# Sliding-window attention units on TensorE: scores ahead of the transposes, one fixed order, steps queued in order

## The chip, the core and the metric

One core of a Trainium2 chip runs one program: TensorE (PE) multiplies, VectorE (DVE) and ScalarE (ACT) do the element-wise work, GpSimd (POOL) small helpers, SyncE (SP) issues the DMAs. The program holds a list of instructions for each engine, with waits on semaphores for what other engines must have finished. The metric is device microseconds of one execution, the median of the runs. The kernel before the change takes 1589.18 us (median of 3 runs, 1588.21 to 1589.36).

## The reference

A decoder block on 1024 tokens of width 1024, in float32:

```python
h = rms_norm(x, ln1_g)
rq, rk, rv, rg, aq, ak, av, gate_a, gate_b = jnp.split(h @ w_in + b_in, SPLIT_IDX, axis=-1)
ry = head_group_norm(retention_chunkwise(rotary(rq), rotary(rk), rv), ret_norm_g)
branch_a = (silu(rg) * ry) @ w_ret_out
ay = sliding_window_sink_attention(rotary(aq), rotary(ak), av, attn_sinks)   # 16 q heads, 2 kv heads of 64
branch_b = ay @ w_attn_out
x = x + (sigmoid(gate_a) * branch_a + sigmoid(gate_b) * branch_b) @ w_out
h2 = rms_norm(x, ln2_g)
x = x + (silu(h2 @ w_ffn_gate) * (h2 @ w_ffn_up)) @ w_ffn_down
return rms_norm(x, lnf_g)
```

The attention works on blocks of 128 queries. A block sees its own 128 keys and the 128 before them (block 0 its own alone), masked to a window of 128, and each head has a learned sink that takes part in the softmax:

```python
m = jnp.maximum(jnp.max(scores, axis=-1, keepdims=True), sink)
e = jnp.exp(scores - m)
probs = e / (jnp.sum(e, axis=-1, keepdims=True) + jnp.exp(sink - m))
out = jnp.einsum('bnhgqk,bnkhd->bnqhgd', probs, vb)
```

## The kernel before, in words

Every float32 operand of a large product is split into a rounded high part and a rest (`split`, `halves`), and a product is three matmuls: high by high, high by low, low by high. The kernel is a row of stages on TensorE: the first norm with k and v, the attention with q's projection and the gates, the retention's v, the retention, the output products, the FFN. The change is in the attention stage alone (L355 to L525, in the trace from about 45 to 357 us).

**The fill.** `quad_q(g)` (L355) projects the queries of four heads (quad g, 0 to 3): 4 products of 24 matmuls of 512 columns, in steps of 3 matmuls (`mm_g`, L148). After each it evicts the bank with an ACT operation (L382); after the third and the fourth it rotates one half of the tokens: six DVE operations, two ACT casts and two DVE rests into the staging tile `stg` (L392 to L401), which goes out to DRAM and comes back in the layout that the scores need, one write (`q_d`, L403) and four reads (L405). `gate(n)` (L482) is a dense product of 48 matmuls, with an ACT tanh (L486) after each half. Weights come by DMA and are split by ACT and DVE (L374, L375 for q; L128, L131 for gates). `Fill` hands these products out a step at a time.

**The units.** There are 32 units (`geo`, L409): unit u is quad u // 8 on block u % 8. A unit has these steps:

- `u_scores` (L417): 8 matmuls of 256 columns, for each of four heads the high and the low part of k against q, into two PSUM tiles "s" (two buffers); by head a DVE operation that adds the mask and takes the row's extreme (L436), and an ACT exponential that sums its row (L439). Then the reciprocal of the sums on DVE (L442), and the scaling of the four heads, two on ACT (L445) and two on DVE (L447).
- `u_transpose` (L451): 8 transposes into two PSUM tiles "t" (two buffers); of each an ACT cast `ph` (L460) and a DVE rest `pl` (L461).
- `u_values` (L464): 4 matmuls of v against `ph` and `pl` into the PSUM tile "pv", which has one buffer. Then two ACT copies (L474, L475) and two DVE additions (L476, L477) out of that bank into `tm`, and an ACT cast and a DVE rest into q's tile (L479, L480).

For block 0 of a quad the scores have 128 columns and there is one transposed tile. The loop (L500) has 33 iterations. Iteration i does `u_transpose(i - 1)`, `u_scores(i)` with all its DVE and ACT work, six or seven steps of fill, and `u_values(i - 1)`. After the loop 120 matmuls of gates remain (`fl.rest()`).

**What sets the order.** The program is traced in that order, and a scheduler then orders each engine's instructions by priority, under their dependencies. `in_order(engines)` (L102) is a context that ties each instruction of an engine to the one traced before it, so that the scheduler can't move them against each other. Before, the attention stage is outside any such context.

Of the kernel before, what the change touches and what calls it, by code (L numbers as in the profile page):

```python
# [2 lines left out]

# [11 lines left out]
ALU = mybir.AluOpType  # L15
# [8 lines left out]
AHEAD = 100  # L24
WARM1 = 30
# [7 lines left out]
def f32(t):  # L33
    return t.bitcast(F32)
# [3 lines left out]
def hybrid_block(ctx: ExitStack, tc: tile.TileContext, x, ln1_g, w_in, b_in, ret_norm_g, w_ret_out,  # L38
# [139 lines left out]

    class Fill:
# [104 lines left out]
    with tc.tile_pool(name="gt", bufs=1, side="right") as gt, tc.tile_pool(name="w1", bufs=1) as w1:  # L284
# [73 lines left out]
        def quad_q(g):  # L358
# [19 lines left out]
            for z, half in ((0, 0), (0, 1), (1, 0), (1, 1)):  # L378
                pt = acc(f"aq{g}{z}{half}")
                yield from mm_g(pt, w[z], H, half * 512)  # L380
                t = r512("ra" if z == 0 else "rb", 2 - z, f"q{g}{z}{half}")
                nc.scalar.activation(t, pt, AF.Identity, bias=bcol[:, QB + 4 * z + g:QB + 4 * z + g + 1], scale=1.0)  # L382
                ab[z, half] = t
                if z == 0:
                    yield
                    continue
                c = slice(half * 512, half * 512 + 512)
                a, b = ab[0, half], t
                stg = w1.tile([P, 4, 512], F32, tag="stg", bufs=1, name=f"stg{g}{half}")
                s0, s1, s2, s3 = (stg[:, i, :] for i in range(4))  # L390
                cos, sin = atab[:, 0, c], atab[:, 1, c]
                nc.vector.tensor_tensor(out=s2, in0=a, in1=cos, op=ALU.mult)  # L392
                nc.vector.tensor_tensor(out=s1, in0=b, in1=sin, op=ALU.mult)
                nc.vector.tensor_tensor(out=s2, in0=s2, in1=s1, op=ALU.subtract)
                nc.vector.tensor_tensor(out=s0, in0=a, in1=sin, op=ALU.mult)
                nc.vector.tensor_tensor(out=s3, in0=b, in1=cos, op=ALU.mult)
                nc.vector.tensor_tensor(out=s3, in0=s3, in1=s0, op=ALU.add)
                nc.scalar.activation(s0.bitcast(F32R), s2, AF.Copy)
                nc.vector.tensor_tensor(out=s2.bitcast(F32R), in0=s2, in1=s0, op=ALU.subtract)
                nc.scalar.activation(s1.bitcast(F32R), s3, AF.Copy)  # L400
                nc.vector.tensor_tensor(out=s3.bitcast(F32R), in0=s3, in1=s1, op=ALU.subtract)  # L401
                qd = q_d[2 * g + half]
                nc.sync.dma_start(qd, stg)  # L403
                for r in range(4):
                    nc.sync.dma_start(f32(Bt[r * 32:r * 32 + 32, jb:jb + 4, c]),  # L405
                                      qd[:, r, :].rearrange("(j e) c -> e j c", e=32))
# [7 lines left out]
        scs = {}  # L414
        phs = {}

        def u_scores(u):  # L417
# [5 lines left out]
            scs[u] = sc  # L423
            nc.gpsimd.tensor_copy(sc[:, :, nk:nk + 1], nsink[:, 4 * g:4 * g + 4].rearrange("p (j o) -> p j o", o=1))  # L424
            nm = tiny.tile([P, 4], F32, tag="nm", name=f"nm{g}{b}")
            den = tiny.tile([P, 4], F32, tag="den", name=f"den{g}{b}")
            for jp in range(2):
# [6 lines left out]
                for jj in range(2):  # L434
                    j = 2 * jp + jj
                    nc.vector.tensor_tensor_reduce(out=sc[:, j, 0:nk], in0=pt[:, jj * 256:jj * 256 + nk], in1=mk,  # L436
                                                   scale=1.0, scalar=nsink[:, 4 * g + j:4 * g + j + 1],
                                                   op0=ALU.add, op1=ALU.min, accum_out=nm[:, j:j + 1])
                    nc.scalar.activation(sc[:, j, 0:nk + 1], sc[:, j, 0:nk + 1], AF.Exp, scale=-1.0,  # L439
                                         bias=nm[:, j:j + 1], accum_out=den[:, j:j + 1])  # L440
            rd = tiny.tile([P, 4], F32, tag="rd", name=f"rd{g}{b}")
            nc.vector.reciprocal(rd, den)  # L442
            for j in range(4):
                if j % 2:
                    nc.scalar.activation(sc[:, j, 0:nk], sc[:, j, 0:nk], AF.Copy, scale=rd[:, j:j + 1])  # L445
                else:
                    nc.vector.tensor_scalar(out=sc[:, j, 0:nk], in0=sc[:, j, 0:nk], scalar1=rd[:, j:j + 1],  # L447
                                            scalar2=None, op0=ALU.mult)

        def u_transpose(u):  # L450
            g, b, nk, Bt, jb, qc = geo(u)  # L451
            sc = scs.pop(u)
            phs[u] = []
            for kb in range(nk // P):
# [5 lines left out]
                nc.scalar.copy(ph, pt)  # L460
                nc.vector.tensor_tensor(out=pl, in0=pt, in1=f32(ph), op=ALU.subtract)  # L461
                phs[u].append((ph, pl))

        def u_values(u):  # L464
# [7 lines left out]
            pvv = pv.rearrange("p (i z q) -> p i z q", i=2, z=2)  # L472
            tm = w1.tile([P, 2, P], F32, tag="tm", bufs=1, name=f"tm{g}{b}")
            nc.scalar.copy(tm[0:64], pvv[64:128, :, 0, :])  # L474
            nc.scalar.copy(tm[64:128], pvv[0:64, :, 1, :])  # L475
            nc.vector.tensor_tensor(out=tm[0:64], in0=pvv[0:64, :, 0, :], in1=tm[0:64], op=ALU.add)  # L476
            nc.vector.tensor_tensor(out=tm[64:128], in0=pvv[64:128, :, 1, :], in1=tm[64:128], op=ALU.add)  # L477
            v = Bt[:, jb:jb + 4, qc].rearrange("p (i z) q -> p i z q", z=2)
            nc.scalar.copy(v[:, :, 0, :], tm)  # L479
            nc.vector.tensor_tensor(out=v[:, :, 1, :], in0=tm, in1=f32(v[:, :, 0, :]), op=ALU.subtract)  # L480
# [19 lines left out]
        for i in range(NU + 1):  # L500
            if i % NB == 0 and 0 < i < NU:
                fl.until(3 * (i // NB - 1) + 1)
            if i > 0:
                u_transpose(i - 1)
            if i < NU:
                u_scores(i)
            fl.step((i + 1) * left // (NU + 1) - i * left // (NU + 1))
            if i > 0:
                u_values(i - 1)
                if i % 4 == 0:  # L510
                    g, b, _, Bt, jb, _ = geo(i - 1)
                    c = slice((b // 4) * 512, (b // 4) * 512 + 512)
                    nc.sync.dma_start(ay_d[g, :, :, c], f32(Bt[:, jb:jb + 4, c]))
            if i == 2 * NB + 4:
                wv = act.tile([P, 16, 512], F32, tag="B", name="wv")
                for q in range(4):
                    nc.sync.dma_start(wv[:, 4 * q:4 * q + 4, :],
                                      w_in[(q // 2) * 512:(q // 2) * 512 + 512, C_RV + (q % 2) * 512:
                                           C_RV + (q % 2) * 512 + 512].rearrange("(k p) n -> p k n", p=P))
            if i > 3 * NB and i % 2:  # L520

                k = (i - 3 * NB) // 2
                nc.vector.tensor_tensor(out=wv[:, 4 + k, :], in0=wv[:, 12 + k, :], in1=wv[:, 4 + k, :],
                                        op=ALU.subtract)
        fl.rest()  # L525
# [1121 lines left out]
```

## Time and profile before

| | |
|---|---|
| median of 3 runs | 1589.18 us |
| the profiled execution | 1587.27 us |
| its span, first to last instruction | 1585.5 us |
| TensorE busy | 1569.7 us |
| VectorE busy | 995.4 us |
| ScalarE busy | 720.2 us |
| mean granted TensorE clock | 0.998 |

The trace covers the profiled execution's span; the 1.8 us beside it lie outside. TensorE's rows need care: a matmul of 512 columns is drawn 0.39 us long, while the next one starts 0.23 us after it, so that a busy TensorE may still be waiting. Start times are exact; ends are modelled.

### The profile page before, as it was taken

What the parts mean: (1) busy time and instruction counts of PE and PEld (TensorE: products, weight loads), DVE (VectorE), ACT (ScalarE), POOL (GpSimd) and SP (SyncE); (2) the same over time, 40 slices, a digit from 0 to 9 for tenths busy, and PEclk for the clock granted to TensorE, in tenths of its full rate; (3) what the DMA queues carried; (4) which work ended last, traced back from release to release, by engine and by line L of the source; (5) the groups of instructions that cost most, each with busy time, mean ns of one, the idle gap of its engine ahead of it and who ended that gap; (6) DMA issues with size and microseconds to landing.
All of it is one profiled execution on the core that took longest, in us unless ns stands there. A gap on an engine that the chain in (4) does not pass through costs nothing.

```text
span 1585.5 us, 20874 instructions
## 1 busy us (share of the span) xinstructions
PE 1569.7 (99%) x7483; PEld 1306.8 (82%) x7483; DVE 995.4 (63%) x1773; ACT 720.2 (45%) x1446; POOL 362.3 (23%) x308
## 2 busy tenths in 40 slices
PE   9999999999999999999999999999999999999998
PEld 8887888888888888888888888888888888788886
DVE  6459978787657663878544368444444444778656
ACT  5258877844233333544221256333333333344445
POOL 2000000000045441000000013555555555200001
PEclk9999999999999999999999999999999999999999
DMA  6564654440364455654545102333333333862333
GB/s 203 161 170 124 206 190 151 145 140 34 126 226 148 134 166 186 231 184 160 176 150 194 54 0 79 101 108 111 108 100 104 107 109 100 306 226 86 99 104 123
DMA packets 148886, 223.13 MB, mean 141 GB/s; under 512 B 9195, under 2 KB 81709, under 8 KB 147246
## 3 DMA queue, kind: packets, MB, share of 16 engines
q1 hardware_dynamic: 148782, 221.80, 43.1%
q8 instruction: 59, 0.97, 0.2%
q14 instruction: 45, 0.37, 0.1%
HBM read 149.67 MB, written 67.37 MB: 137 GB/s over the span
## 4 chain that ended last, share of the span: by engine, by line
PE 88%; ACT 5%; DVE 5%; issue 1%; DMA 0%; POOL 0%; POOLq 0%; SPq 0%; DVEq 0%; ACTq 0%
PE fA L1310 15%; PE fB L1310 8%; PE dA L1571 7%; PE wA L814 7%; PE dxP L1571 6%; PE fC L1310 4%; PE wB L814 3%; PE va L659 3%; PE vP L659 2%; ACT sc L439 2%; PE acc_g L155 2%; PE acc_g L156 2%; PE wo L1248 2%; PE wo L1249 2%; PE acc_ba L156 2%; PE acc_ba L157 2%
## 5 line engine op out<-in xcount | busy, mean ns | idle before, releaser
L1571 PE MATMUL dA<-dwP,daP 128*128 128x512 f32 x528 | 121.4, 390 | 0.8 <-DVE xf L1347 0.8
L1571 PEld LDWEIGHTS dA<-dwP,daP 128*128 128x128 f32 x528 | 98.8, 188 | 22.7 <-DVE xf L1347 1.2
L1571 PE MATMUL dxP<-dwP,daP 128*128 128x512 f32 x396 | 90.2, 389 | 0.0
L1571 PEld LDWEIGHTS dxP<-dwP,daP 128*128 128x128 f32 x396 | 74.3, 188 | 15.4
L424 POOL COPY sc<-nsink 128x4 f32<-128x4 f32 x32 | 12.7, 399 | 275.2 <-PE pT L457 147.4
L1368 POOL TENSOR_TENSOR xf<-xf 128x512 f32<-128x512 f32 x44 | 67.9, 1543 | 33.0 <-issue 30.1
L156 PE MATMUL acc_g<-h,wh_g 128*128 128x512 f32 x192 | 75.4, 393 | 0.0
L155 PE MATMUL acc_g<-h,wh_g 128*128 128x512 f32 x192 | 75.3, 392 | 0.0
L157 PE MATMUL acc_g<-h,wl_g 128*128 128x512 f32 x192 | 75.2, 392 | 0.0
L439 ACT ACTIVATE sc<-sc,nm 128x257 f32<-128x257 f32 (+1 forms) x128 | 62.5, 492 | 26.0 <-DVE nm L436 25.6
L1321 POOL TENSOR_TENSOR xf<-xf 128x512 f32<-128x512 f32 x33 | 49.3, 1493 | 54.5 <-ACT t_1P L128 22.4
L436 DVE CUSTOM_DVE_ANT_0 sc<-s,amask,nsink 128x256 f32<-128x256 f32 (+1 forms) x128 | 54.1, 461 | 9.5 <-PE s L433 9.2
L1331 ACT COPY xf<-fA 128x512 f32<-128x512 f32 x44 | 25.7, 586 | 74.3 <-PE fA L1310 74.3
L131 DVE TENSOR_TENSOR dwP<-wd,dwP 128x512 fp32r<-128x512 f32 x77 | 56.0, 728 | 4.6 <-ACT dwP L128 4.6
L128 ACT CAST dwP<-wd 128x512 fp32r<-128x512 f32 x77 | 47.4, 615 | 12.4 <-PE dA L1571 9.9
L155 PE MATMUL acc_bb<-ay,wh_bb 128*128 128x512 f32 x128 | 50.9, 399 | 0.0
L156 PE MATMUL acc_bb<-ay,wh_bb 128*128 128x512 f32 x128 | 50.3, 393 | 0.0
L156 PE MATMUL aq<-h,wh_aq 128*128 128x512 f32 x128 | 50.2, 392 | 0.0
L155 PE MATMUL aq<-h,wh_aq 128*128 128x512 f32 x128 | 50.1, 391 | 0.0
L1489 POOL TENSOR_TENSOR rs_f<-tot,mhalf 128x1 f32<-128x1 f32 x8 | 4.8, 605 | 198.0 <-DVE tot L1486 198.0
L157 PE MATMUL acc_bb<-ay,wl_bb 128*128 128x512 f32 x128 | 50.0, 391 | 0.0
L157 PE MATMUL aq<-h,wl_aq 128*128 128x512 f32 x128 | 50.0, 392 | 0.0
(799 smaller groups left out, 4395.5 us busy)
## 6 DMA issues: line engine op xcount, KB each, us to landing
act_d<-xf SPq DMA_DIRECT2D x77, 256.0 KB, 2.1
daP<-act_d SPq DMA_DIRECT2D x21, 512.0 KB
q_d<-stg SPq DMA_DIRECT2D x8, 1024.0 KB
q<-q_d SPq DMA_DIRECT2D x32, 256.0 KB, 6.2
ay_d<-q SPq DMA_DIRECT2D x8, 1024.0 KB
ay<-ay_d SPq DMA_DIRECT2D x4, 2048.0 KB, 13.9
wr_daP<-act_d SPq DMA_DIRECT2D x14, 512.0 KB, 3.9
wr_g<-in_w_in SPq DMA_DIRECT2D x12, 512.0 KB, 5.9
```

Of the source, the lines that this page charges most:

```text
L131: nc.vector.tensor_tensor(out=lo, in0=raw, in1=f32(hi), op=ALU.subtract)
L155: nc.tensor.matmul(pt, hi[:, k, :], xh, start=(k == 0), stop=False)
L156: nc.tensor.matmul(pt, hi[:, k, :], xl, start=False, stop=False)
L157: nc.tensor.matmul(pt, lo[:, k, :], xh, start=False, stop=(k == 7))
L436: nc.vector.tensor_tensor_reduce(out=sc[:, j, 0:nk], in0=pt[:, jj * 256:jj * 256 + nk], in1=mk, scale=1.0, scalar=nsink[:, 4 * g + j:4 * g ...
L439: nc.scalar.activation(sc[:, j, 0:nk + 1], sc[:, j, 0:nk + 1], AF.Exp, scale=-1.0, bias=nm[:, j:j + 1], accum_out=den[:, j:j + 1])
L659: nc.tensor.matmul(vbanks[pr][tt], x_[:, c], w[:, u, :], start=(fresh and k + z == 0), stop=(k == 3 and z == 2), skip_group_check=not fresh)
L814: nc.tensor.matmul(pt, o[:, w, k, :], v, start=(first and k + z == 0), stop=(k == 3 and z == 2), skip_group_check=not first)
L1310: nc.tensor.matmul(pt, o[:, w, k, :], v, start=(first and k + z == 0), stop=(k == 3 and z == 2), skip_group_check=not first)
L1321: nc.gpsimd.tensor_tensor(out=dst[q], in0=dst[q], in1=sg[q], op=ALU.mult)
L1368: nc.gpsimd.tensor_tensor(out=o, in0=a, in1=b, op=op)
L1571: nc.tensor.matmul(banks[tt], a[:, u, c], w[:, v, :], start=(fresh and f + z == 0), stop=(f == NP - 1 and z == 2), skip_group_check=not fresh)
```

## The change

Six edits, all in the attention stage.

1. The loop runs in `in_order(nc.tensor.engine)`: TensorE keeps the traced order.
2. Iteration i now traces `u_scores(i)`, one step of fill (`FIRST`), `u_transpose(i - 1)`, `u_scale(i)`, `u_out(i - 2)`, the other steps of fill, and `u_values(i - 1)`.
3. `u_scale` is the second half of the old `u_scores` (reciprocal and scaling); `u_out` is the second half of the old `u_values` (all that reads the bank "pv"). It is traced an iteration later than before, behind the scaling of the unit two further on.
4. Each DVE and ACT operation of a unit goes through `queued`, which ties it to the engine's queued operation before it. Evictions, splits and the rotation are not tied.
5. The rotation of quads 1 to 3 is put in a list, `beside`, and one entry is issued after each step of fill; the write and reads through DRAM come with the last entry. Quad 0 is rotated at once, as before.
6. The write of four finished blocks (`ay_d`) is issued from `u_out`.

```diff
+        def queued(x):
+
+            i = x.ins
+            if i.engine in queues:
+                tc.add_manual_dep(i, queues[i.engine],
+                                  mybir.DependencyInfo(mybir.DependencyClass.NoSync, mybir.DependencyReason.DATA),
+                                  reason="queued")
+            queues[i.engine] = i.name
...
                 try:
                     next(self.gens[0])
                     n -= 1
+                    if beside:
+                        beside.pop(0)()
...
+                todo = [partial(mix, s2, a, cos, ALU.mult), partial(mix, s1, b, sin, ALU.mult),
+                        partial(mix, s2, s2, s1, ALU.subtract), partial(mix, s0, a, sin, ALU.mult),
+                        partial(mix, s3, b, cos, ALU.mult), partial(mix, s3, s3, s0, ALU.add),
+                        partial(hl, s2, s0), partial(hl, s3, s1), ship]
+                if g == 0:
+                    for f in todo:
+                        f()
+                else:
+                    beside.extend(todo[:-2] + [lambda x=todo[-2], y=todo[-1]: (x(), y())])
...
+        def u_out(u):
+            g, b, nk, Bt, jb, qc = geo(u)
+            pvv = pvs.pop(u).rearrange("p (i z q) -> p i z q", i=2, z=2)
             tm = w1.tile([P, 2, P], F32, tag="tm", bufs=1, name=f"tm{g}{b}")
...
+            queued(nc.scalar.copy(tm[0:64], pvv[64:128, :, 0, :]))
+            queued(nc.scalar.copy(tm[64:128], pvv[0:64, :, 1, :]))
+            queued(nc.vector.tensor_tensor(out=tm[0:64], in0=pvv[0:64, :, 0, :], in1=tm[0:64], op=ALU.add))
+            queued(nc.vector.tensor_tensor(out=tm[64:128], in0=pvv[64:128, :, 1, :], in1=tm[64:128], op=ALU.add))
...
+        with in_order(nc.tensor.engine):
+            for i in range(NU + 1):
+                n = (i + 1) * left // (NU + 1) - i * left // (NU + 1)
+                if i % NB == 0 and 0 < i < NU:
+                    fl.until(3 * (i // NB - 1) + 1)
+                if i < NU:
+                    u_scores(i)
+                if i > 0:
+                    fl.step(FIRST)
+                    u_transpose(i - 1)
+                if i < NU:
+                    u_scale(i)
+                if i > 1:
+                    u_out(i - 2)
+                fl.step(n - FIRST if i > 0 else n)
+                if i > 0:
+                    u_values(i - 1)
...
+            u_out(NU - 1)
+            fl.rest()
```

In the rows of the program below a name carries the quad and the block: `sc34` is the score tile of quad 3, block 4 (unit 28), `pv33` the value bank of the unit before it. Rows of the changed program have its own line numbers.

TensorE before, from the values of unit 26 to the fill after the scores of unit 28: `pv` are values, `pT` transposes, `s340` and `s341` the two score tiles, `acc_g13` the fill.

```order
L470 MATMUL pv32_3259<-ph321_3196,vst_169 128x512
L471 MATMUL pv32_3259<-pl321_3197,vst_169 128x512
L457 MATMUL pT330_3272<-ident_81,sc33_3200 128x128 x4
L457 MATMUL pT331_3281<-ident_81,sc33_3200 128x128 x4
L432 MATMUL s340_3294<-kst_168,q2_1418 128x256
L433 MATMUL s340_3294<-kst_168,q2_1418 128x256
```

TensorE in the changed program at the same place:

```order
L499 MATMUL pv32_3259<-ph321_3214,vst_169 128x512
L500 MATMUL pv32_3259<-pl321_3215,vst_169 128x512
L457 MATMUL s340_3269<-kst_168,q2_1418 128x256
L458 MATMUL s340_3269<-kst_168,q2_1418 128x256
...
L160 MATMUL acc_g13_0_3243<-h1_112,wl_g13_3240 128x512
L486 MATMUL pT330_3290<-ident_81,sc33_3175 128x128 x4
L486 MATMUL pT331_3299<-ident_81,sc33_3175 128x128 x4
```

The scores of unit 28 now stand directly behind the values of unit 26, and one step of fill is between them and the transposes of unit 27; 18 matmuls of fill and the values of unit 27 follow.

ScalarE before, in the iterations of unit 27 and 28: exponentials and scaling (`sc`), copies out of the value bank (`tm`), casts of the transposed tiles (`ph`), the last cast (`q2`), a gate's tanh (`tb`).

```order
L445 ACTIVATE sc33_3200<-sc33_3200,rd33_3222 128x256 x2
L474 COPY tm32_3264<-pv32_3259 64x256
L475 COPY tm32_3264<-pv32_3259 64x256
L460 CAST ph330_3277<-pT330_3272 128x512
L460 CAST ph331_3286<-pT331_3281 128x512
L479 CAST q2_1418<-tm32_3264 128x2x128
L439 ACTIVATE sc34_3290,den34_3293<-sc34_3290,nm34_3292 128x257 x4
L486 ACTIVATE tb130_3327<-acc_g13_0_3243,bhalf_87 128x512
L445 ACTIVATE sc34_3290<-sc34_3290,rd34_3312 128x256 x2
```

ScalarE in the changed program, the iteration of unit 28:

```order
L464 ACTIVATE sc34_3265,den34_3268<-sc34_3265,nm34_3267 128x257 x4
L489 CAST ph330_3295<-pT330_3290 128x512
L489 CAST ph331_3304<-pT331_3299 128x512
L522 ACTIVATE tb130_3327<-acc_g13_0_3243,bhalf_87 128x512
L474 ACTIVATE sc34_3265<-sc34_3265,rd34_3308 128x256 x2
L507 COPY tm32_3314<-pv32_3259 64x256
L508 COPY tm32_3314<-pv32_3259 64x256
L512 CAST q2_1418<-tm32_3314 128x2x128
```

The copies of unit 26's values (`tm32`) stood ahead of the exponentials of unit 28; they now stand behind them, behind the casts of unit 27 and behind unit 28's scaling. VectorE has the same order: its additions of `tm32` (L509, L510) follow unit 28's four reductions (L461), unit 27's two rests (L490), unit 28's reciprocal (L471) and its scaling (L476).

VectorE in the changed program where a rotation meets the units, between the end of iteration 2 and the third reduction of iteration 3 (`stg11` is the rotation of quad 1's second half, `tm00` the end of unit 0, `sc03` and `nm03` unit 3's reductions):

```order
L510 TENSOR_TENSOR tm00_1055<-pv00_1002,tm00_1055 64x256
L402 TENSOR_TENSOR stg11_989<-q101_852,atab_164 128x512
L402 TENSOR_TENSOR stg11_989<-q111_987,atab_164 128x512
L513 TENSOR_TENSOR q0_627<-tm00_1055,q0_627 128x2x128
L402 TENSOR_TENSOR stg11_989<-stg11_989 128x512
L402 TENSOR_TENSOR stg11_989<-q101_852,atab_164 128x512
L402 TENSOR_TENSOR stg11_989<-q111_987,atab_164 128x512
L461 ISA sc03_1100,nm03_1102<-s030_1104,amask_166,nsink_85 128x256
L461 ISA nm03_1102 128x1
L402 TENSOR_TENSOR stg11_989<-stg11_989 128x512
L461 ISA sc03_1100,nm03_1102<-s030_1104,amask_166,nsink_85 128x256
```

Five rotation operations stand between unit 0's last use of the value bank and unit 3's first reduction, a sixth behind that. Two rests of the rotation (L406) follow ahead of unit 3's fourth reduction.

Unit 0's scores stand, in the changed program, behind 156 matmuls of q's projection; before they stood behind all 192 of quads 0 and 1 and 41 matmuls of a gate.

More of the change, by code (lines that the diff above doesn't have):

```diff
@@ L2 @@
 from contextlib import ExitStack, contextmanager
+from functools import partial
 import numpy as np
@@ L24 @@
 AHEAD = 100
+FIRST = 1
 WARM1 = 30
@@ L177, in dense @@
         run(dense_g(src, col, X, evac, name))
+    beside = []
     class Fill:
@@ L391, in quad_q @@
                 cos, sin = atab[:, 0, c], atab[:, 1, c]
[L392 to L406, printed above, removed]
+                def mix(o, p, q, op):
+                    nc.vector.tensor_tensor(out=o, in0=p, in1=q, op=op)
@@ new lines, in hl, with ship @@
+                def hl(v, hi):
+                    nc.scalar.activation(hi.bitcast(F32R), v, AF.Copy)
+                    nc.vector.tensor_tensor(out=v.bitcast(F32R), in0=v, in1=hi, op=ALU.subtract)
+                def ship(qd=q_d[2 * g + half], stg=stg, Bt=Bt, jb=jb, c=c):
+                    nc.sync.dma_start(qd, stg)
+                    for r in range(4):
+                        nc.sync.dma_start(f32(Bt[r * 32:r * 32 + 32, jb:jb + 4, c]),
+                                          qd[:, r, :].rearrange("(j e) c -> e j c", e=32))
@@ L426, in u_scores @@
             den = tiny.tile([P, 4], F32, tag="den", name=f"den{g}{b}")
+            scs[u] = sc, den
             for jp in range(2):
@@ L499, in hybrid_block @@
         left = 32 * 8 - 8 - 20
[L500 to L524, printed above, removed]
```

56 lines of the change are left out of this document (33 added, 23 removed).

## Prediction

> **What bounds the kernel now.** I read the page first, then the chain of waits, TensorE's waits in the attention stage, that stage's windows, and the timeline of one regular stretch.
>
> ```profile
> span 1585.5 us, 20874 instructions
> PE 1569.7 (99%) x7483; PEld 1306.8 (82%) x7483; DVE 995.4 (63%) x1773; ACT 720.2 (45%) x1446; POOL 362.3 (23%) x308
> ```
>
> TensorE is the bound, and the change takes no matmul away. All it can win is time in which TensorE waits. The windows, with the attention stage as 100 to 330 us (columns: busy time of PE, PEld, DVE, ACT, POOL, then the granted clock):
>
> ```profile
> 0.00:40.00 40.00, 36.42 (x267) 32.99 (x268) 26.44 (x46) 23.24 (x41) 11.72 (x25) 0.96 0.61 205
> 100.00:330.00 230.00, 226.62 (x1208) 187.58 (x1208) 194.01 (x574) 189.72 (x528) 12.39 (x30) 1.00 0.52 161
> ```
>
> TensorE shows 3.4 us idle in the stage, with 84% of VectorE and 82% of ScalarE used. The modelled ends hide more: a 512-column row is drawn 0.39 us and the next starts 0.23 us on, so each wait may hide 0.16 us; with two waits a unit at most, 64 x 0.16 = 10.2 us, which makes 3.4 to 13.6 us. I take 8 us as what the old order loses, the middle.
>
> The late part of the stage is regular. TensorE's rows there, unit 27's values to unit 28's:
>
> ```profile
> 301.27 0.40 PE L470 MATMUL pv<-ph,vst 128*128 128x512 f32 x1
> ...
> 303.20 0.28 PE L433 MATMUL s<-kst,q 128*128 128x256 f32 x1
> ...
> 303.91 0.28 PE L433 MATMUL s<-kst,q 128*128 128x256 f32 x1
> ...
> 308.81 0.40 PE L470 MATMUL pv<-ph,vst 128*128 128x512 f32 x1
> ...
> 309.74 1.03 PE L457 MATMUL pT<-ident,sc 128*128 128x128 f32 x8
> ```
>
> An iteration takes 308.81 - 301.27 = 7.54 us, and 0.93 of it (308.81 to 309.74) are the four value matmuls. TensorE does not wait there. So in the new order, with the same work, TensorE would come to the values 7.54 - 0.93 = 6.61 us after the first score matmul.
>
> **The change part by part.** *The order and the moved output step (edits 1 to 4).* The values of unit i-1 write the one bank "pv". In iteration i the old contents, unit i-2's, are read by two ACT copies and two DVE additions, and the rows of the order put these behind unit i's exponentials and scaling. Unit i's exponentials need unit i's scores, and TensorE's next scores now come behind these values. That closes a ring: scores of i, softmax of i, output of i-2, values of i-1, scores of i+1. If it is longer than 7.54 us, it sets the pace, and with TensorE's order fixed no fill can slip in. I add it up from the start of the scores, taking starts of rows that follow each other.
>
> ```profile
> 100.94 0.28 PE L433 MATMUL s<-kst,q 128*128 128x256 f32 x1
> ...
> 101.26 0.48 DVE L436 CUSTOM_DVE_ANT_0 sc<-s,amask,nsink 128x256 f32<-128x256 f32 x1 [0.30 <-PE s L433]
> ...
> 102.27 0.17 DVE L442 RECIPROCAL rd<-den 128x4 f32<-128x4 f32 x1
> ...
> 102.47 0.70 ACT L445 ACTIVATE sc<-sc,rd 128x128 f32<-128x128 f32 x2
> ```
>
> ```profile
> 302.78 0.36 ACT L475 COPY tm<-pv 64x256 f32<-64x256 f32 x1
> 303.17 1.07 ACT L460 CAST ph<-pT 128x512 fp32r<-128x512 f32 x2
> 303.18 0.42 DVE L476 TENSOR_TENSOR tm<-pv,tm 64x256 f32<-64x256 f32 x1 [1.55 <-ACT tm L475]
> 303.61 0.43 DVE L477 TENSOR_TENSOR tm<-pv,tm 64x256 f32<-64x256 f32 x1
> 304.07 0.69 DVE L461 TENSOR_TENSOR pl<-pT,ph 128x512 fp32r<-128x512 f32 x1
> 304.13 0.42 ACT L479 CAST q<-tm 128x256 fp32r<-128x256 f32 x1
> 304.67 0.42 DVE L480 TENSOR_TENSOR q<-tm,q 128x256 fp32r<-128x256 f32 x1
> 305.61 0.48 DVE L436 CUSTOM_DVE_ANT_0 sc<-s,amask,nsink 128x256 f32<-128x256 f32 x1
> 306.19 0.51 ACT L439 ACTIVATE sc<-sc,nm 128x257 f32<-128x257 f32 x1 [1.64 <-DVE nm L436]
> 308.18 0.67 ACT L486 ACTIVATE tb<-acc_g,bhalf 128x512 f32<-128x512 f32 x1
> 308.75 0.90 ACT L445 ACTIVATE sc<-sc,rd 128x256 f32<-128x256 f32 x2
> 309.55 1.03 ACT L128 CAST wh_g<-wr_g 128x1024 fp32r<-128x1024 f32 x1
> 310.60 0.37 ACT L474 COPY tm<-pv 64x256 f32<-64x256 f32 x1
> 310.98 0.37 ACT L475 COPY tm<-pv 64x256 f32<-64x256 f32 x1
> ```
>
> - Scores run 0.118 us apart (303.20 to 303.91, six steps). The fourth closes the first score tile: 3 x 0.118 + 0.28, and 0.04 to the DVE (101.22 to 101.26). First reduction at 0.67.
> - First exponential 0.58 later (305.61 to 306.19): 1.25. Four take 1.99 of ACT (306.19 to 308.18): 3.24. Unit i-1's transposes are long done.
> - The casts `ph` of unit i-1: ACT is free 0.96 later (303.17 to 304.13), the first is done after 0.59 (1.07 less the 0.48 step). First rest `pl` at 3.24 + 0.59 + 0.04 = 3.87. Two rests of 0.60 (304.07 to 304.67): the reciprocal of unit i starts at 5.07.
> - 0.20 to ACT's scaling (102.27 to 102.47): 5.27. Two scalings 0.80 (308.75 to 309.55): 6.07. Two copies, 0.38 (310.60 to 310.98) and 0.36: 6.81.
> - 0.04 (303.14 to 303.18), two additions of 0.43: 7.71.
>
> From there to TensorE there is one row pair, which ends one of TensorE's own waits:
>
> ```profile
> 145.14 0.44 DVE tm L477
> ...
> 145.71 0.47 PE pv L470
> ```
>
> That is 0.13 us after the addition's end (145.58): the values start at 7.84, where TensorE could at 6.61. The iteration takes 7.84 + 0.93 = 8.77 us in place of 7.54: 1.23 us more. Thirty iterations (2 to 31) have the ring. In six it is lighter (three with 128-column scores, three with one transposed tile); between 0 and 1.23 I take half. 24 x 1.23 + 6 x 0.62 = 33.2 us. Iterations 11 and 22 have six steps of fill, so TensorE arrives 3 x 0.227 = 0.68 us earlier for nothing: 1.4 more, 34.6 us. An error of 0.25 us in the ring is 7 us.
>
> *The rotation (edit 5).* Six halves of eight DVE operations at 0.60 us:
>
> ```profile
> 104.61 0.60 DVE stg L396
> 105.22 0.60 DVE pl L461
> ```
>
> That is 28.8 us of VectorE if all of it lay on the ring, and 0 if all of it fell into VectorE's pauses there. Worked for iteration 2 into 3 by the order's rows: after the second addition (7.71) stand five rotations and unit 0's last rest, 5 x 0.60 + 0.35, so unit 3's first reduction can start at 11.06, where the ring wants it at 8.77 + 0.67 = 9.44: 1.6 us late. Three more stand between its four reductions, 1.8 us. So 3.4 us a quad, 10 us in three; other places fall into the pause ahead of `pl` and cost nothing.
>
> *Other fill on the ring.* Evictions and weight splits aren't tied, but take their place in the lists. A tanh (0.57, 308.18 to 308.75) between the casts and the scaling fits into ACT's pause there (3.24 + 0.96 = 4.20 to 5.27); a pair of weight splits of quads 2 and 3 doesn't always. Four such pairs at up to 1.2 us and some eight evictions at 0.57: 0 to 9.4 us. I take 6.
>
> *Unit 0 earlier.* Its scores now stand 36 matmuls ahead of the end of quad 1's projection.
>
> ```profile
> 77.00 1.77 SPq L405 DMA_DIRECT2D q<-q_d  x4
> ```
>
> ```profile
> 89.67 0.39 PE L157 MATMUL aq<-h,wl_aq 128*128 128x512 f32 x1
> ```
>
> ```profile
> q<-q_d SPq DMA_DIRECT2D x8, 256.0 KB, 6.2
> ```
>
> The row at 89.67 is the last of the 192, so TensorE reaches unit 0 at 89.90 - 36 x 0.227 = 81.7. The four reads of q were issued from 77.0 to 78.8, the last at about 78.3, and land 6.2 us later: 84.5. The DMA queue ahead of them is unchanged. A wait of 2.8 us that was not there (0 to 4). Later quads have whole iterations of cover, and edit 6 has the 120 gate matmuls behind the loop (120 x 0.227 = 27 us).
>
> Sum: 34.6 + 10 + 6 + 2.8 - 8 = +45 us. The profiled execution's 1587.3 becomes 1632; the median lies 1.9 above it, so **1634 us**.
>
> One rule of the Trainium skill speaks of such waits. The rows first: the granted clock is 0.96 in the first 40 us, where TensorE idles 3.6 us, and 1.00 in the stage with its short waits. "TensorE: Matmul & The Clock Gate", section "HAM oscillation", warns of idle gaps over about 3.4 us, after which the clock is halved for a window. By that rule the ring's 1.23 us is harmless, and only iterations like 3 (1.2 + 3.4) would lose half of such a window, a further 1.7 us each, an estimate of 3 to 5 us in all and a time of about 1638; no run shown so far has such a gap, and none of it is in the sum.
>
> **The rivals.**
>
> *A, faster: the ring is shorter than 6.61 us.* Then TensorE never waits for the bank, the 8 us go, unit 0 costs 2.8: 1589.2 - 5.2 = 1584 us. For it: VectorE idles 1.55 us and ScalarE 1.64 us in the regular stretch, so the engines have room. Against: these are pauses in sequence; ACT's own work from the first exponential to the last copy is 1.99 + 0.96 + 0.80 + 0.74 = 4.5 us, and with the 1.25 before and the 1.03 behind it 6.8, without any pause for `pl`. It decides if my sum is 1.23 too long. Chance 0.09.
>
> *B, the ring binds lightly.* At 7.0 in place of 7.84 it costs 30 x 0.4 = 12, with fill in the pauses, unit 0 at 2.8, less 8: +7, about 1596 us. It needs handoffs half as long as the rows show. Chance 0.09, of which half lies within 0.2% of the old time if the old waits were nearer 13.6.
>
> *C, VectorE binds.* With the rotation all on the ring: +19 on the forecast, 1653 us. Chance 0.07.
>
> That the change does not do what it says is excluded by the rows of the order.
>
> **How the numbers follow.** The forecast has 0.75; slower takes in C and half of B: 0.75 + 0.07 + 0.045, rounded 0.87; faster 0.09; same 0.04. (0.2% of this time, 3.2 us, is about what a measurement can tell.) The range: below, 27 (ring 0.25 shorter) + 2 - 13.6 = +15, 1604; above, 42 + 20 + 6 + 2.8 - 3.4 = +67, 1656. It holds the forecast's 0.75 and most of C.
>
> **What would show it.** Right: TensorE's waits led by the first value matmul on the second addition, about 30 times and 1.2 us each; the regular iteration at 8.8 us; ScalarE's copies of unit i-2 behind the scaling of unit i; one wait of unit 0's scores on q's reads near 82 us; the stage some 45 us longer, all after it only shifted. Wrong: iterations of 7.5 us, or waits that sit on the transposes in place of the values, would say that the ring isn't there; long waits on first reductions behind rotations would say that VectorE's load, not the ring, is the price.

## The result and the profile after

The changed kernel takes 1651.57 us (median of 4 runs, 1650.68 to 1651.73), the kernel before 1588.89 us in the same job (4 runs, 1588.21 to 1589.36): a ratio of 1.04, 95% interval 1.0388 to 1.0413. The profiled execution's span is 1649.8 us, 64.3 more than before.

The page, then TensorE's waits (us in all, times, the longest):

```profile
span 1649.8 us, 20928 instructions
PE 1582.7 (96%) x7483; PEld 1316.0 (80%) x7483; DVE 994.2 (60%) x1773; ACT 723.3 (44%) x1446; POOL 358.9 (22%) x308
```

```profile
PE pv L499 <- DVE tm L510: 48.8, 29, 4.4
PE s L457 <- DMA q<-q_d: 3.3, 1, 3.3
```

One wait carries nearly all: the first value matmul on the second addition out of the bank "pv", 29 times. The same stage's windows as before, with the stretch around unit 0 ahead of them (busy time of PE, PEld, DVE, ACT, POOL, then the granted clock):

```profile
80.00:100.00 20.00, 16.72 (x71) 13.78 (x70) 12.54 (x34) 8.56 (x25) 0.19 (x1) 0.83 0.79 210
100.00:330.00 230.00, 191.21 (x967) 156.98 (x966) 155.27 (x443) 148.10 (x403) 6.43 (x24) 0.96 0.42 135
```

VectorE and ScalarE are less used than before (155 and 148 us of 230, against 194 and 190): neither is full, they wait for each other. And the granted clock, 1.00 in this stage before, is 0.96. A regular iteration:

```profile
351.89 0.47 PE L499 MATMUL pv<-ph,vst 128*128 128x512 f32 x1 [1.71 <-DVE tm L510]
...
352.89 0.28 PE L457 MATMUL s<-kst,q 128*128 128x256 f32 x1
...
353.67 0.48 DVE L461 CUSTOM_DVE_ANT_0 sc<-s,amask,nsink 128x256 f32<-128x256 f32 x1 [1.03 <-PE s L458]
...
354.26 0.51 ACT L464 ACTIVATE sc<-sc,nm 128x257 f32<-128x257 f32 x1 [2.08 <-DVE nm L461]
...
356.25 1.05 ACT L489 CAST ph<-pT 128x512 fp32r<-128x512 f32 x2
...
356.85 1.29 DVE L490 TENSOR_TENSOR pl<-pT,ph 128x512 fp32r<-128x512 f32 x2 [1.47 <-ACT ph L489]
...
358.05 0.17 DVE L471 RECIPROCAL rd<-den 128x4 f32<-128x4 f32 x1
...
358.31 0.91 ACT L474 ACTIVATE sc<-sc,rd 128x256 f32<-128x256 f32 x2 [0.43 <-DVE rd L471]
...
359.25 0.37 ACT L507 COPY tm<-pv 64x256 f32<-64x256 f32 x1
...
360.02 0.42 DVE L509 TENSOR_TENSOR tm<-pv,tm 64x256 f32<-64x256 f32 x1 [1.16 <-ACT tm L508]
...
360.45 0.43 DVE L510 TENSOR_TENSOR tm<-pv,tm 64x256 f32<-64x256 f32 x1
...
361.03 0.47 PE L499 MATMUL pv<-ph,vst 128*128 128x512 f32 x1 [1.35 <-DVE tm L510]
```

Read down, this is the ring step by step: each row waits for the one above it or stands behind it in its engine's queue. Once around takes 361.03 - 351.89 = 9.14 us, where an iteration took 7.54 before. There are two kinds of loss in it: the wait itself, and what follows some of the longer waits. TensorE behind the pause that ends at 294.90:

```profile
294.90 0.64 PE L499 MATMUL pv<-ph,vst 128*128 128x512 f32 x1 [3.76 <-DVE tm L510]
295.34 0.63 PE L500 MATMUL pv<-pl,vst 128*128 128x512 f32 x1
295.76 0.63 PE L499 MATMUL pv<-ph,vst 128*128 128x512 f32 x1
...
298.32 0.45 PE L158 MATMUL acc_g<-h,wh_g 128*128 128x512 f32 x1
298.61 0.40 PE L159 MATMUL acc_g<-h,wh_g 128*128 128x512 f32 x1
298.85 0.40 PE L160 MATMUL acc_g<-h,wl_g 128*128 128x512 f32 x1
```

From 294.90 to 298.32 the matmuls run at half rate: the 512-column ones start 0.42 us apart in place of 0.24 behind that.

**Where the time went.** I take every step between starts of TensorE's rows from 60 to 420 us, less its regular length (0.227 us behind 512 columns, 0.118 behind 256, 0.11 behind a transpose). Steps some 0.2 us too long (0.1 for the short ones) that come five or more in a row are "half rate"; the number of such stretches is in brackets. "Ahead of values" is what stands ahead of a unit's first value matmul; waits ahead of its three others are under "all other".

| us | time | ahead of values | unit 0's scores | half rate | all other | sum |
|---|---|---|---|---|---|---|
| before | 1588.9 | 1.4 | 0 | 0 | 9.7 | 11.1 |
| changed | 1651.6 | 53.8 | 3.4 | 11.8 (6) | 4.2 | 73.2 |

The sums differ by 62.1 us, the medians by 62.7, so nearly the whole difference lies in this stage. Of the 64.3 us between the two profiled executions 2.0 lie ahead of it: the first product of q's projection starts at 47.79 us in place of 45.76, and the granted clock over the first 40 us is 0.91 in place of 0.96.

### The profile page after: what moved, and what is told of

It reads as the page before. It is cut to its first block, busy times and chain, and to the rows that moved or that the text cites. A ratio compares the mean times of both kernels' runs of the same rounds, so it can differ in the third digit from the quotient of the medians.

```text
span 1649.8 us, 20928 instructions
## 1 busy us (share of the span) xinstructions
PE 1582.7 (96%) x7483; PEld 1316.0 (80%) x7483; DVE 994.2 (60%) x1773; ACT 723.3 (44%) x1446; POOL 358.9 (22%) x308
## 4 chain that ended last, share of the span: by engine, by line
PE 83%; ACT 6%; DVE 6%; issue 2%; DMA 2%; SPq 0%; POOL 0%; ACTq 0%; POOLq 0%; DVEq 0%
PE fA L1350 14%; PE fB L1350 7%; PE dA L1611 7%; PE wA L854 6%; PE dxP L1611 5%; PE fC L1350 4%; PE wB L854 3%; PE va L699 3%; PE vP L699 2%; PE wo L1290 2%; PE acc_ba L158 2%; PE acc_ba L160 2%; PE wo L1289 2%; PE wo L1288 2%; PE acc_ba L159 2%
## 5 line engine op out<-in xcount | busy, mean ns | idle before, releaser
L464 ACT ACTIVATE sc<-sc,nm 128x257 f32<-128x257 f32 (+1 forms) x128 | 62.1, 487 | 67.3 <-DVE nm L461 67.3
L448 POOL COPY sc<-nsink 128x4 f32<-128x4 f32 x32 | 7.9, 249 | 340.6 <-PE pT L486 160.1
L499 PE MATMUL pv<-ph,vst 128*128 128x512 f32 x60 | 27.0, 450 | 48.9 <-DVE tm L510 48.8
L461 DVE CUSTOM_DVE_ANT_0 sc<-s,amask,nsink 128x256 f32<-128x256 f32 (+1 forms) x128 | 52.8, 464 | 26.5 <-PE s L458 26.2
L490 DVE TENSOR_TENSOR pl<-pT,ph 128x512 fp32r<-128x512 f32 x60 | 38.8, 686 | 39.0 <-ACT ph L489 38.8
L499 PEld LDWEIGHTS pv<-ph,vst 128*128 128x128 f32 x60 | 11.6, 193 | 62.2 <-ACT tm L508 43.1
L158 PE MATMUL aq<-h,wh_aq 128*128 128x512 f32 x128 | 52.6, 411 | 0.0
L159 PE MATMUL aq<-h,wh_aq 128*128 128x512 f32 x128 | 51.3, 401 | 0.0
L158 PE MATMUL acc_bb<-ay,wh_bb 128*128 128x512 f32 x128 | 50.9, 399 | 0.0
```

The source lines that it names most:

```text
L158: nc.tensor.matmul(pt, hi[:, k, :], xh, start=(k == 0), stop=False)
L159: nc.tensor.matmul(pt, hi[:, k, :], xl, start=False, stop=False)
L461: queued(nc.vector.tensor_tensor_reduce(out=sc[:, j, 0:nk], in0=pt[:, jj * 256:jj * 256 + nk], in1=mk, scale=1.0, scalar=nsink[:, 4 * g + ...
L464: queued(nc.scalar.activation(sc[:, j, 0:nk + 1], sc[:, j, 0:nk + 1], AF.Exp, scale=-1.0, bias=nm[:, j:j + 1], accum_out=den[:, j:j + 1]))
```

## The experiments

Twelve runs, in four jobs. The kernel before took 1589.07 us in the first, 1587.8 to 1588.0 in the others. Each edit is against the changed kernel if nothing else is said.

**Two value banks** (`banks`): odd units' values go into a bank of the fill's pool.

```diff
-            pv = ps("pv", 1, f"pv{g}{b}")
+            pv = ps("pv", 1, f"pv{g}{b}") if u % 2 == 0 else acc(f"pv{g}{b}")
```

> The changed kernel with a second value bank: odd units write their values into one of the three banks of the fill's products, so that the values of unit i-1 wait for the output of unit i-3 and no longer for that of unit i-2. TensorE's order is the same word for word. The ring theory (the bank closes a ring through the softmax of the next unit but one): the 48.8 us of waits of the value matmuls on the second addition go, and with them most of the slow-clock matmuls behind the long waits, some 8 us; left are unit 0's wait of 3.3 us and what was lost before. 1651.6 - 49 - 8 gives 1595 us, 1585 to 1605. The rival that VectorE's and ScalarE's load, with the rotation in it, sets the pace whatever bank is free: the waits move to the rests and scalings, and it stays above 1630 us.

Measured: 1617.9 us, ratio 1.0189 (1.0172 to 1.0206), less than the changed kernel by 33.7 us and more than the theory had. TensorE's waits, then the start of one iteration:

```profile
PE pv L499 <- ACT ph L489: 9.1, 9, 1.8
PE pv L500 <- DVE pl L490: 5.4, 20, 0.6
```

```profile
321.11 0.28 PE L457 MATMUL s<-kst,q 128*128 128x256 f32 x1
...
321.29 0.91 ACT L474 ACTIVATE sc<-sc,rd 128x256 f32<-128x256 f32 x2
...
322.23 0.37 ACT L507 COPY tm<-pv 64x256 f32<-64x256 f32 x1
...
323.89 0.41 ACT L512 CAST q<-tm 128x256 fp32r<-128x256 f32 x1 [0.92 <-DVE tm L510]
...
324.33 0.42 DVE L513 TENSOR_TENSOR q<-tm,q 128x256 fp32r<-128x256 f32 x1 [0.47 <-ACT q L512]
...
324.78 0.48 DVE L461 CUSTOM_DVE_ANT_0 sc<-s,amask,nsink 128x256 f32<-128x256 f32 x1
...
329.64 0.28 PE L457 MATMUL s<-kst,q 128*128 128x256 f32 x1
```

The waits on the additions are gone: the bank's ring was real. But an iteration still takes 8.53 us. Scores that begin at 321.11 could be reduced 0.7 us later; the first reduction starts at 324.78. Ahead of it in VectorE's queue stand the additions and the rest of the older unit's output, which wait for ScalarE's copies and cast, and these for the scaling. So a second ring lies under the first and has no bank in it: scaling, copies, additions, cast, rest, next reductions, exponentials, casts, rests, next scaling, handed to and fro between two engines that keep their order.

**The output at once again** (`now`), tied as it is, right behind its own unit's values; and **between scores and transposes** (`early`).

```diff
-                if i > 1:
-                    u_out(i - 2)
...
                     u_values(i - 1)
+                    u_out(i - 1)
```

> The changed kernel with one step put back: each unit's output step is issued behind its values, as in the kernel before, with the one value bank; TensorE's order, the queued steps and the spread rotation stay. The ring theory: the output is then over 1.9 us behind the values and no softmax is in its way; the softmax starts 1.9 us later and the rests end at about 7.2 us after the scores, where the last value matmul needs them at 7.3. So TensorE hardly waits in a plain iteration, but has little slack: 1590 to 1605 us. The rival of the engines' load: still above 1630 us.

```diff
                 if i < NU:
                     u_scores(i)
+                if i > 1:
+                    u_out(i - 2)
                 if i > 0:
                     fl.step(FIRST)
```

> The changed kernel with the output step of unit i-2 put between unit i's exponentials and the casts of unit i-1's transposes; all else as changed. The ring theory: the bank comes free about 5.1 us after the scores in place of 8.0, ahead of the values at 6.6, but the rests of unit i-1 now end at about 7.3, so that the fourth value matmul waits 0.1 to 0.5 us in an iteration: 1595 to 1612 us. The rival of the engines' load: above 1630 us.

Measured: 1623.22 us, 1.0216 (1.0201 to 1.0232), and 1620.78 us (one run). Both miss their range by over 8 us. TensorE's waits in `now`:

```profile
PE pv L499 <- ACT ph L489: 11.0, 11, 2.8
PE pv L500 <- DVE pl L490: 7.2, 24, 1.1
```

At three tied places the output costs 32 to 63 us over before; earlier helps, but where it is tied to stand ahead of the next unit's work, that work waits instead. In `now`, scores that begin at 318.06 meet a VectorE whose queue holds the older unit's additions and its rest, which waits for ScalarE's cast; the first reduction starts at 321.34, directly behind that rest.

**The rotation in one heap** (`rot`): edit 5 undone.

```diff
-                if g == 0:
+                if g >= 0:
```

> The changed kernel with the rotation of all quads issued at once, as in the kernel before (edit 5 undone); the ring stays. The ring theory: the plain iteration stays at 9.1 us and the waits on the second addition stay near 49 us, 5 more or less, since the same 48 operations come in other places: 1640 to 1660 us. The rival that the spread rotation is the price: 1610 to 1630 us.

Measured: 1664.82 us (one run), 13 more than the changed kernel, just above the range. The pauses ahead of the values grow by only 2.8 us in all (56.6 against 53.8), but are less even, up to 5.2 us, and the stretches at half rate go from 6 to 11: 21.0 us in place of 11.8. So 9.2 of the 13 us hang on which pauses are followed by half rate, and in a single execution that is in part chance (see below).

**No ties** (`noq`), and **no ties with two banks** (`banks_noq`).

```diff
-            if i.engine in queues:
+            if False:
```

> The changed kernel without the ties among the units' VectorE and ScalarE operations; TensorE's order and the one bank stay. Theory (two rings: the bank, and under it the tied order of the two queues, in which the casts ph of unit i-1 stand behind all four exponentials of unit i): with the ties gone casts and rests may go ahead of the next unit's exponentials, both rings get shorter, 1595 to 1625 us, and TensorE's waits on VectorE's additions are under half of the 48.8 us. Rival one (the traced order alone sets the queues, the ties add nothing): 1648 to 1655, waits as before. Rival two (without the ties the output of unit i-2 drifts behind evictions and rotation): over 1660.

> Two value banks and no ties; TensorE's order, the later output and the spread rotation stay. Theory (two rings): both are gone, what is left is unit 0's wait on q's reads (3.4 us, some 3 more at a lower clock) and a little more: 1588 to 1602 us, and TensorE's waits for casts and rests (14.5 us with two banks and the ties) are under 6 us. Rival one (with two banks it is the fixed order of TensorE alone that still waits for the transposes' casts, whatever the two queues do): 1613 to 1621, the same as two banks with the ties. Rival two (VectorE's load): the same 1613 to 1621, with waits on VectorE's rests.

Measured: 1599.97 us, 1.0076 (1.006 to 1.0091), and 1588.47 us, 1.0002 (0.9993 to 1.0011). Both lie in the theory's ranges. With two banks TensorE's waits are:

```profile
PE s L457 <- DMA q<-q_d: 3.5, 1, 3.5
PE pv L500 <- DVE pl L490: 2.1, 3, 1.2
```

So fixing TensorE's order with the scores ahead costs nothing on balance here, once the two other queues and the bank let it run.

**The spread rotation alone, in the kernel before** (`before_rot`), and **TensorE's fixed order alone, in the kernel before** (`before_pe`): `with in_order(nc.tensor.engine):` around the old loop.

```diff
+                    if beside:
+                        beside.pop(0)()
...
+                if g == 0:
+                    for f in todo:
+                        f()
+                else:
+                    beside.extend(todo[:-2] + [lambda x=todo[-2], y=todo[-1]: (x(), y())])
```

> The kernel before with the spread rotation alone. If spreading saves here too (undoing it in the changed kernel cost 13 us), by taking the eight VectorE operations out of one heap: 1578 to 1586 us, at most the 8 us that the old order was said to lose. If the 13 us were only the ring's (a heap of rotations delays a ring that already sets the pace) and the old order, in which fill covers them, loses nothing to it: 1587 to 1591. If each entry of the rotation issued between steps of fill is in the units' way: 1592 to 1600.

> The kernel before with one edit alone: TensorE's traced order held (transposes of i-1, scores of i, fill, values of i-1), the output read out of the bank at once. If the queues' order and the bank are the whole price: unit 0's wait on q's reads is all that is left of the change, 3 to 7 us, 1589 to 1597 us. If holding TensorE's order is itself a price, since fill can no longer slip in where a unit's step is late: 1600 to 1625, with waits spread over casts, rests and scaled scores.

Measured: 1586.74 us, 0.9993 (0.9984 to 1.0002), no difference: in the old order it is the same whether the rotation is spread or not, and the 13 us belong to the kernel with the ring; and 1606.18 us, 1.0116 (1.0102 to 1.0131), the second reading. The waits of `before_pe`:

```profile
PE pT L457 <- DVE sc L447: 8.8, 6, 3.8
PE pT L457 <- ACT sc L445: 4.0, 4, 2.9
```

In the old traced order (transposes, then scores) a fixed TensorE waits for the scaled scores, where the free one before took fill. No wait of a transpose on a scaled score is among the changed kernel's: with the scores ahead of the transposes, the scaling is done when TensorE comes to them.

**Only the output untied** (`out_free`), with one bank and with two (`banks_out_free`): of the units' operations the six of `u_out` go without `queued`, all others stay tied.

```diff
-            queued(nc.scalar.copy(tm[0:64], pvv[64:128, :, 0, :]))
+            nc.scalar.copy(tm[0:64], pvv[64:128, :, 0, :])
...
```

> The changed kernel with the six operations of the output (two copies, two additions, cast and rest of q) not tied; reductions, exponentials, casts, rests and scalings stay tied, as do TensorE's order and the one bank. With all ties off the time was 1600.0 us. Theory (the place of the output is the whole price of the ties: tied, its copies stand behind the scaling of the unit two further on, and its last two operations ahead of the next unit's reductions): 1597 to 1607 us. Rival (the ties among reductions, exponentials, casts and scalings cost as well, for a pair of splits or an eviction can no longer be passed): 1615 to 1640, with waits for casts and rests.

> Two value banks and the output's six operations not tied, all else as changed. Two banks with the ties took 1617.9, without any tie 1588.5 us. Theory (the second ring, too, closes through the output: scaling, copies, additions, cast and rest of q, next unit's reductions, each waiting for the other engine): 1587 to 1597 us. Rival (the second ring is the casts of unit i-1 behind the exponentials of unit i, which stay tied): 1608 to 1620, with TensorE's waits on casts and rests at 14 us as with two banks and all ties.

Measured: 1593.33 us, 1.0034 (1.0022 to 1.0047), less than the theory had, and 1593.33 us, 1.0036 (1.0023 to 1.005), in its range. Untying six operations out of twenty-three gives back 58.2 of the 62.7 us, and a second bank adds nothing to it. `out_free`'s waits ahead of the values, beside unit 0's, and one iteration:

```profile
PE pv L499 <- ACT ph L489: 1.9, 2, 1.2
PE pv L499 <- DVE tm L510: 1.8, 2, 1.6
```

```profile
316.06 0.48 DVE L461 CUSTOM_DVE_ANT_0 sc<-s,amask,nsink 128x256 f32<-128x256 f32 x1 [1.05 <-PE s L458]
...
317.69 0.42 DVE L509 TENSOR_TENSOR tm<-pv,tm 64x256 f32<-64x256 f32 x1
...
318.12 0.43 DVE L510 TENSOR_TENSOR tm<-pv,tm 64x256 f32<-64x256 f32 x1
...
321.91 0.40 PE L499 MATMUL pv<-ph,vst 128*128 128x512 f32 x1
...
323.04 0.37 ACT L507 COPY tm<-pv 64x256 f32<-64x256 f32 x1 [0.85 <-PE pv L500]
...
323.62 0.48 DVE L461 CUSTOM_DVE_ANT_0 sc<-s,amask,nsink 128x256 f32<-128x256 f32 x1 [2.17 <-PE s L458]
```

Left free, the scheduler puts the copies ahead of the next exponentials, into ScalarE's pause while TensorE computes the scores (323.04), and the additions behind the four reductions, into VectorE's pause while ScalarE takes the exponentials (317.69). The bank is free at 318.55, 3.4 us before the values at 321.91, and the iteration is 7.56 us again (316.06 to 323.62).

**Unit 0 later** (`banks_noq_late`): 18 matmuls of the fill move ahead of unit 0, on top of `banks_noq`.

```diff
-        fl.step(20)
-        left = 32 * 8 - 8 - 20
+        fl.step(26)
+        left = 32 * 8 - 8 - 26
```

> Two value banks, no ties, and unit 0's scores 18 matmuls (4.1 us) later in the fill; TensorE's order and the spread rotation stay. Without the last edit 1588.5 us, with one wait of 3.6 us for q's reads and some eight matmuls at half rate behind it (2 us). Theory (that wait and the half rate behind it are all that is left of the change's price): the wait is gone, 1581.5 to 1585 us, faster than both kernels. Rival (18 matmuls less of fill for the units make other waits): 1586 to 1591, with new waits before the values or behind the loop.

Measured: 1588.98 us, 1.0006 (0.9997 to 1.0016): the rival was right.

```profile
PE pv L500 <- DVE pl L490: 3.8, 3, 2.8
PE pT L486 <- DVE sc L476: 2.5, 1, 2.5
```

The wait on q's reads is gone, but unit 0's transposes now wait 2.5 us for its scaling, with a few matmuls at half rate behind that (0.43 us apart from 97.30 to 99.01), and one unit's values wait 2.8 for a rest; TensorE's pauses sum to 10.9 us, against 10.4 without this edit and 11.1 before the change. No version here is faster than the kernel before by more than the measurement can tell.

**The output untied and the rotation in one heap** (`out_free_rot`): both edits above.

> The changed kernel with the output's six operations not tied (1593.3 us) and, besides, the rotation issued in one heap again as before. Undoing the spreading alone, with the ties, cost 13 us, and the heap's iterations there had pauses of 3.5 to 5.2 us ahead of the values. Theory (a heap costs only where the ring already sets the pace): 1590 to 1597 us. Rival (eight VectorE operations in one heap delay the fixed order of TensorE whatever the output does): 1602 to 1610, with pauses over 3 us in the three iterations with a heap.

Measured: 1594.58 us, 1.0043 (1.0026 to 1.006), against 1593.33 with the spread rotation. Outside a ring the heap costs next to nothing.

The same account of TensorE's pauses for the runs that decide (of the 21.2 us under "all other" with two banks, 15.1 are ahead of a unit's later value matmuls, where it waits for casts and rests):

| us | time | ahead of values | unit 0's scores | half rate | all other | sum |
|---|---|---|---|---|---|---|
| two banks | 1617.9 | 11.8 | 3.5 | 3.6 (3) | 21.2 | 40.2 |
| no ties | 1600.0 | 10.3 | 3.7 | 7.2 (3) | 1.9 | 23.1 |
| output untied | 1593.3 | 4.3 | 3.5 | 2.9 (2) | 4.9 | 15.6 |
| two banks, no ties | 1588.5 | 0.0 | 3.6 | 1.5 (1) | 5.2 | 10.4 |
| before, fixed TensorE | 1606.2 | 0.0 | 3.6 | 7.1 (4) | 19.7 | 30.3 |
| rotation in one heap | 1664.8 | 56.6 | 3.6 | 21.0 (11) | 5.1 | 86.3 |

## Why the prediction was right, and by how much it missed

The forecast was 1634 us; 1651.6 were measured, 17.6 more. Step by step:

- **The ring: right in place and mechanism, a little short.** 29 waits of the first value matmul on the second addition, the copies behind the scaling of the unit two further on, 9.14 us a plain iteration against 8.77. Measured from the first score matmul (352.89), the first reduction starts at 0.78 (forecast 0.67), the first exponential at 1.37 (1.25), the rests at 3.96 (3.87), the scaling at 5.42 (5.27), the copies at 6.36 (6.07, ScalarE's two scalings with their handoffs take 0.94, not 0.80), the additions at 7.13 (6.85), the values at 8.14 (7.84). The four value matmuls take 1.00, not 0.93.
- **Rotation and other fill: about right together.** Ring, rotation and fill were put at 34.6 + 10 + 6 = 50.6 us; the pauses ahead of the values are 53.8. With the plain ring at 1.5 us of pause (24 x 1.5, six at half, and 1.4 as in the forecast: 41.9) some 12 remain for rotation and fill, forecast 16. That the total comes so near is in part luck: the plain ring was put 7 us too low, and rotation and fill 4 too high. The iteration worked out in the prediction came as told, with rotations (L402) and their rests (L406) ahead of and between the reductions of unit 3:

```profile
112.18 1.28 DVE L402 TENSOR_TENSOR stg<-q,atab 128x512 f32<-128x512 f32 x2
...
113.50 0.48 DVE L461 CUSTOM_DVE_ANT_0 sc<-s,amask,nsink 128x256 f32<-128x256 f32 x1
...
113.91 0.69 DVE L402 TENSOR_TENSOR stg<-stg 128x512 f32<-128x512 f32 x1
...
115.32 1.29 DVE L406 TENSOR_TENSOR stg<-stg 128x512 fp32r<-128x512 f32 x2
...
116.53 0.48 DVE L461 CUSTOM_DVE_ANT_0 sc<-s,amask,nsink 128x256 f32<-128x256 f32 x1
...
122.33 0.77 PE L499 MATMUL pv<-ph,vst 128*128 128x512 f32 x1 [4.41 <-DVE tm L510]
```

  Its pause is 4.6 us, 3.1 over the plain 1.5, where 3.4 was forecast. But the prediction booked this under edit 5, the spreading. The runs correct that: the rotation lies on the ring in either form, spreading it went with 13 us less there (`rot`, one execution, 9.2 of them half rate) and with next to nothing elsewhere (none in `before_rot`, 1.3 us in `out_free_rot`).
- **Unit 0's scores: right.** 3.4 us against 2.8.
- **The old waits: nearly.** Of 8 us that were to go, 5.5 went: the pauses at all other places fell from 9.7 to 4.2 us.
- **The half rate: the term that failed.** It was left out of the sum, with 3 to 5 us beside it; it is 11.8, two thirds of the miss. The rows of the windows are above (0.96 over the stage, 0.83 around unit 0), and six stretches follow the waits that end at 87.25, 122.33, 236.23, 273.09, 294.90 and 332.39. Three of them follow pauses of only 2.1 to 2.4 us, and two of these (236.23 and 332.39) stand in iterations without any rotation. By the Trainium skill ("TensorE: Matmul & The Clock Gate", section "HAM oscillation"), gaps over about 3.4 us bring the half rate. The stretch shown above lasts 3.42 us, as long as the window that page gives (3.4 us), but the threshold does not hold here: 2.1 us was enough at 332.39. Nor does the length alone decide: a pause of 3.0 us in `out_free_rot` (at 257.48) left the next values 0.23 to 0.31 us apart, at full rate. The same page, section "What's actually happening", says that the window runs free of the program. The traces agree: in each run the granted clock changes only on a grid of 3.413 us. In the changed kernel the half rate of this stage begins at 86.82, 120.95, 237.00, 274.55, 295.03 and 332.58, which are 10, 34, 11, 6 and 11 such steps apart, and from run to run the grid lies elsewhere against the program, 0.1 to 2.7 us behind the span's start. What counts is how much pause falls into one window of this grid (in these rows PE's busy time, the second number, is 3.41 us in a window without a pause, and hides some 0.16 us of each pause; the clock stands third from the end):

```profile
329.17:332.58 3.41, 1.50 (x7) 0.97 (x6) 1.87 (x6) 1.95 (x5) 0.00 (x0) 1.00 0.00 0
332.58:335.99 3.41, 3.41 (x13) 3.01 (x13) 2.00 (x8) 1.09 (x5) 0.00 (x0) 0.50 0.50 195
148.26:151.67 3.41, 1.99 (x9) 1.31 (x7) 2.34 (x6) 2.78 (x7) 0.00 (x0) 1.00 0.23 62
151.67:155.08 3.41, 2.29 (x14) 2.09 (x15) 1.76 (x6) 0.50 (x2) 0.00 (x0) 1.00 1.05 328
155.08:158.49 3.41, 3.41 (x21) 2.87 (x20) 1.95 (x9) 3.03 (x10) 0.19 (x1) 1.00 0.00 0
```

  The pause of 2.1 us that ends at 332.39 lies whole in one window, and the next window is at half rate. The pause of 2.7 us that ends at 152.79 is longer, but the grid cuts it at 151.67 into 1.6 and 1.1 us, and no half rate follows; that of 3.0 us in `out_free_rot` is cut into 1.8 and 1.3. In the changed kernel six windows at full rate hold over 2.0 us of pause in all, and half rate follows each of them; no other is followed by it, and the fullest of these holds 1.96 us. In `rot` it is eleven windows, and 1.88 us. So for pauses of 2 to 3 us it is chance whether they cost twice.
- **The rivals.** A and B fell with the ring. C's time (1653) is nearest to the measured one, but not its mechanism: VectorE is busy 155 of 230 us, less than before, and TensorE's waits don't lie on reductions.
- **What the prediction did not see** cost it nothing, but would have misled a repair: it took 7.54 us for what an iteration needs once the bank is free. Under the bank's ring stood the second one of 8.53 us through the same tied output. A second bank alone gives back 33.7 of 62.7 us; untying the output opens both rings. Which of its six ties matters most was not tried: with the output traced early but tied (`now`) copies stand ahead of the next exponentials on ScalarE as in `out_free`, and it still takes 1623 us, which points to the additions ahead of the reductions and to the cast and rest ahead of the next unit's softmax. One iteration of its trace, told above, has just that; how much each tie costs is not shown.

## What to carry to other kernels

When queues are fixed in order, follow one iteration's work from engine to engine until it comes back to where it began: the longest such loop is the pace, however idle every engine is, and opening one loop shows the next. Tie only what has to be tied: a piece of work with slack, such as an output, is worth most when it may fall into whichever pause comes. And a wait of TensorE can cost more than its length, so look at the start distances behind it too.

## What the runs showed of the hardware

Pauses of TensorE of 2.1 to 4.6 us were followed by stretches of 11 to 18 matmuls in the changed kernel at half rate (0.427 us between 512-column matmuls in place of 0.227), about 2 us lost each time: 6 of them in the changed kernel and 11 in `rot`, which makes 9.2 of the 13 us between these two. Others of the same length were followed by none: 2.7 us at 152.79 and 197.74 in the changed kernel. In these runs it was not the length of a pause that decided: the granted clock changed only at the ends of windows of 3.413 us, which lay in each run at another place against the program, and it fell to half after a window with about 2 us of pause in it. Over this stage in all fourteen traces no window at full rate with more than 2.04 us went without half rate behind it, and none with less than 1.83 us had it.
